# A residual-network trunk in float32: half of the down projection's low weight parts by a negated copy and an accumulating DMA

## The chip, the cores and the metric

The kernel runs on one core of one Trainium2 chip. The metric is the time of one execution in microseconds (us) on the device. Before the change it is 2249.22 us, the median of three runs (2248.68 to 2249.78).

## The reference

Two decoder layers over 256 tokens of 2048 channels, all in float32. Each layer normalises its input, projects it once for two kinds of attention, adds the output projection to the residual stream, and then adds an MLP. The change lies in the last line, the down projection of the MLP.

```python
def hybrid_layer(x, ...):
    h = rms_norm(x, attn_norm)
    proj = jnp.einsum('bsd,de->bse', h, w_in)
    ...
    mixed = jnp.concatenate([o_gla, o_sb], axis=-1)
    x = x + jnp.einsum('bse,ed->bsd', mixed, w_o)
    hm = rms_norm(x, mlp_norm)
    up = jnp.square(jax.nn.relu(jnp.einsum('bsd,df->bsf', hm, w_up)))   # 2048 -> 8192
    return x + jnp.einsum('bsf,fd->bsd', up, w_down)                    # 8192 -> 2048
```

## The kernel before

All weights (about 400 MB) stream once from HBM through SBUF. TensorE works on a float32 format with fewer bits (`F32R`), so every weight is split into a high part (the value rounded to that format) and a low part (what the rounding left). Activations are split in the same way, and a product is made of three matmuls: high by high, high activation by low weight, low activation by high weight.

`weight_parts` (L307) makes the split. It loads one **group** of weights, 1 MB, with one DMA on SP's queue into a tile `raw` of 128 partitions by 2048 float32 values (L314; three such buffers). Then it goes through the group's two halves, 128x1024 values each. For a half, ScalarE copies `raw` into `whi`, which rounds (L325), and VectorE subtracts `whi` from `raw` into `wlo` (L327, two sources). There are four buffers of `whi` and four of `wlo`, handed out in turn. It is a generator: each half is given to its caller before the next one is made.

`unit` (L332) makes a product of 256 tokens by 512 columns. It walks over four groups of weights, 512 rows each. For each half it issues 12 matmuls of 512 columns (L344 to L346), so 24 for a group. `unit_t` (L378) is the same with the columns on partitions; the up projection uses it.

`mlp_down` (L902) calls `unit` four times for a quarter of the 8192 hidden channels, once for each 512 output columns, and adds the accumulator to the residual stream on VectorE (L919). So one call is a **pass** of 16 groups. A layer has four passes, with up projections between the first three and the next, and there are two layers. The very last pass of the program writes the output and is treated apart in the change.

The order on each engine comes from the program and a scheduler in the framework. An engine takes its instructions in order. A load can be issued when its `raw` buffer is free, that is when everything that reads the former group in it is done. A `whi` or `wlo` can be written when TensorE is done with the half that had the buffer before.

Of the kernel before, what the change touches and what calls it, by code (L numbers as in the profile page):

```python
# [16 lines left out]
P = 128  # L17
# [22 lines left out]
def trunk_kernel(  # L40
# [31 lines left out]
    def nm(s):  # L72
        uid[0] += 1
        return f"{s}_{uid[0]}"
# [16 lines left out]
    def f32(ap):  # L91
        return ap.bitcast(F32)

    nc.scalar.preload_act_table_set("natural_log_exp_and_others")

# [1 line left out]
    ident = cpool.tile([P, P], F32, name="ident")  # L97
# [9 lines left out]
    def build_constants():  # L107
        nc.vector.tensor_copy(ident16, ident)

        # strictly causal mask of a diagonal block, keys on partitions: 0 where s < t  # L110
        nc.gpsimd.memset(mask16, 0.0)
        nc.gpsimd.affine_select(
            out=mask16, in_=mask16, compare_op=ALU.is_gt, fill=NEG,
            base=0, pattern=[[1, P]], channel_multiplier=-1,
        )
        # suffix sums: -1 where j >= s (j on partitions)
        tri_f, nones_f = tmp("t2", [P, P], bufs=4), tmp("t2", [P, P], bufs=4)
        nc.gpsimd.memset(tri_f, -1.0)
        nc.gpsimd.affine_select(
            out=tri_f, in_=tri_f, compare_op=ALU.is_ge, fill=0.0,  # L120
            base=0, pattern=[[-1, P]], channel_multiplier=1,
        )
        nc.vector.tensor_copy(tri, tri_f)
        nc.gpsimd.memset(nones_f, -1.0)
        nc.vector.tensor_copy(nones, nones_f)
        # 1 where s <= c and both lie in one chunk (s on partitions)
        nc.gpsimd.memset(gmask, 1.0)
        for half in range(2):
            nc.gpsimd.affine_select(
                out=gmask[half * CHUNK : (half + 1) * CHUNK, :],  # L130
                in_=gmask[half * CHUNK : (half + 1) * CHUNK, :],
                compare_op=ALU.is_ge, fill=0.0,
                base=0, pattern=[[1, CHUNK]], channel_multiplier=-1,
            )
        # scan multiplier: 0 at the start of each chunk
        nc.gpsimd.memset(reset, 1.0)
        nc.gpsimd.memset(
            reset.rearrange("p (n c) -> p n c", c=CHUNK)[:, :, 0:1], 0.0
        )
        # exp(last - cum) * k, tokens on partitions, one chunk's rows kept per entry  # L140
        nc.gpsimd.memset(kdz, 0.0)

# [1 line left out]
    NA = KT * DEPTH  # L144
# [48 lines left out]

# [1 line left out]
    xb = [xpool.tile([P, NT, 512], F32, name=f"xb{n}") for n in range(4)]  # L195
# [8 lines left out]

# [1 line left out]
    clock = [0]  # L206
# [16 lines left out]

# [1 line left out]
    def inv_rms(ss, n, width):  # L225
        """(ss / width + EPS) ** -0.5, [P, n], with one Newton step."""
        v, y, t, t2, rr = stat(n), stat(n), stat(n), stat(n), stat(n)
        nc.vector.tensor_scalar(v, ss, 1.0 / width, EPS, ALU.mult, ALU.add)
        nc.scalar.activation(y, v, AF.Ln)
        nc.scalar.activation(y, y, AF.Exp, scale=-0.5)  # L230
        nc.vector.tensor_tensor(t, y, y, ALU.mult)
        nc.vector.scalar_tensor_tensor(t2, t, -0.5, v, ALU.mult, ALU.mult)
        nc.vector.scalar_tensor_tensor(rr, t2, 1.5, y, ALU.add, ALU.mult)  # L233
        return rr

    class Operand:
        """Activations with channels on partitions: [P, 2 blocks, (high, low), T] tiles."""

# [14 lines left out]
    def norm_operand(op, n, key, l):  # L253
        """Residual block n -> operand blocks 4n.. (scaled by the gain)."""
        for h2 in range(2):
# [34 lines left out]
    def wait_on_x(n):  # L290
        """Keep the array running while the first operands arrive."""
        pw = ps_tile()
        for _ in range(n):
            nc.tensor.transpose(pw[:, :P], ident, ident)

    def row_of(col):
        """[P, NT] per-token column -> [P, T] rows, the same on every partition."""
        pb = ps_tile()
        for tt in range(NT):
            w = tmp("bc", [P, P], bufs=1)  # L300
            nc.gpsimd.tensor_copy(w, col[:, tt : tt + 1].to_broadcast([P, P]))  # L301
            nc.tensor.transpose(pb[:, tt * P : (tt + 1) * P], w, ident)
        row = tmp("row", [P, T], bufs=2)
        nc.vector.tensor_copy(row, pb[:, :T])
        return row

    def weight_parts(w2d, r0, c0, kt, width, fine=False, halves=1, order=lambda k: None):  # L307
        """kt row blocks from row r0: exact high and low parts, in pieces of row blocks."""
        full = 2048 // kt
# [3 lines left out]
        for s in range(0, kt, step):  # L313
            nc.sync.dma_start(raw[:, s : s + step, :width], src[:, s : s + step, :])  # L314
        for s in range(2):
            hk = kt // 2
            hi = wpool.tile([P, hk, full], F32R, tag="whi", name=nm("whi"), bufs=4)
# [13 lines left out]

    def unit(op, w2d, row0, c0, width, groups=(0, 1, 2, 3), hooks={}, fine=0, split=False, order=lambda i, k: None):  # L332
        """[T, width] = op @ w2d[row0 + ..., c0:c0+width], tokens on partitions."""
        acc = acc_tile()
# [15 lines left out]
        def prep(i):  # L350
            return weight_parts(
                w2d, row0 + 4 * groups[i] * P, c0, 4, width, fine=i < fine,
                halves=2 if fine else 1, order=lambda k: order(i, k),
            )
# [23 lines left out]
    def unit_t(op, w2d, c0):  # L378
        """The same for 256 columns with the columns on partitions.

        acc[:, f, 0:T] holds the high x high products, acc[:, f, T:] the others.
        """
        acc = acc_tile()
# [18 lines left out]
    def join(acc):  # L402
        """unit_t result -> [P, 2, T] on chip."""
        t = tmp("t2", [P, 2, T], bufs=4)
        nc.scalar.activation(t, acc[:, :, T:], AF.Copy)  # L405
        nc.vector.tensor_tensor(t, acc[:, :, :T], t, ALU.add)  # L406
        return t

    def head_sums(ss, src, nh):
        """Sums of squares over each 128 columns of src [P, nh * 128] -> ss [P, nh]."""  # L410
        sq = tmp("t2", [P, 512], bufs=4)
# [12 lines left out]

# [1 line left out]
    def sb_qk(acc, c, nh, h0, rst, scale, dst, wait):  # L426
        """dst[:, h0.., tok] = normalised heads of acc[:, :, c..], channels on partitions."""
        w = nh * P
# [38 lines left out]
    def sb_scores(qT, kT, h):  # L467
        """Heads h, h+1: zA [keys 0-127, (head, T)], zB [keys 128-255, (head, queries 128-255)]."""
        zA, zB = ps_tile(), ps_tile()
# [59 lines left out]
    def norm_pair(po):  # L529
        """A head pair's outputs [P, (head, tok tile, d)], each row normalised."""  # L530
        o = tmp("on", [P, 512], bufs=4)
# [6 lines left out]
    def to_operand(op, i, o, gcol):  # L538
        """Normalised outputs of a head pair -> blocks 2i, 2i+1 of the operand."""
        pt = ps_tile()  # L540
# [17 lines left out]

# [1 line left out]
    hT = Operand()  # L560
# [10 lines left out]
    for l in range(DEPTH):  # L571
# [36 lines left out]
        def sb_heads(g, qT, kT, v, first):  # L608
            """Held work for heads 4g.. ; first: wait for each pair's scores."""
            state = {}  # L610
# [18 lines left out]

        # stick-breaking heads 0-3; the gate's low-rank columns come along  # L630
        uk = unit(hT, wl, 0, C_SK, 512)
# [11 lines left out]

        # gates of the linear attention, channels on partitions
        gt = {}
# [61 lines left out]

        # stick-breaking heads 4-7
        uv = unit(hT, wl, 0, C_SV + 512, 512)
# [8 lines left out]

        # linear attention: q and k with channels on partitions, two heads a block
        eb, enb, ekd = gt["e"]  # L720
# [36 lines left out]
        def gla_pair(e, v, vc):  # L757
            """Heads 2e, 2e+1; their values are columns vc.. of v."""
            pu = ps_tile()
# [98 lines left out]

        # output projection and residual
        def residual(op, n, key, ll, ssq, acc, done):  # L860
# [16 lines left out]

        # MLP
        up = {}
# [22 lines left out]
        def mlp_down(q):  # L902
            for n in range(4):
                end = q == 3 and l + 1 == DEPTH
                ud = unit(
                    up[q], w_down[l], q * KT * P, n * 512, 512, split=(end and n == 3)
                )
# [60 lines left out]
```

## Time and profile before

| | |
|---|---|
| median of three runs | 2249.22 us |
| span of the profiled execution, first to last instruction | 2247.4 us |
| TensorE matmul busy | 2238.0 us |
| VectorE busy | 1315.8 us |
| ScalarE busy | 1085.9 us |
| GpSimd (POOL) busy | 37.7 us |
| DMA, mean | 182 GB/s |

The profile is of one execution. Its own time outside the profiler is not listed; its span stands 1.8 us under the median of the runs, which is what lies around the span. Matmul ends are modelled and overlap, so the time from one matmul's start to the next says more than the duration of one. The share of DMA is the mean share of time in which the core's 16 DMA engines were busy.

### The profile page before, as it was taken

Reading aid. Unit: us, or ns where it says so; the run is one execution under the profiler, and the core shown is the slowest. Engines: PE = TensorE matmul, PEld = TensorE weight load, DVE = VectorE, ACT = ScalarE, POOL = GpSimd, SP = SyncE. Lnnn points to the kernel's source line nnn. Section 1 sums busy time; section 2 is a strip of 40 time slices with the busy share of each in tenths; the row PEclk is TensorE's granted clock in tenths of the full one; section 3 lists DMA queues with packets and bytes.
Section 4 is the critical chain, followed back from the end, with each engine's and each line's share of the span. In section 5 each row is a group of like instructions: output and inputs, shape, how many; then the busy total and the mean of one; then the engine's idle time right before and its main releaser. Section 6 shows DMA issues by size and latency. Waiting matters only on the chain.

```text
span 2247.4 us, 28019 instructions
## 1 busy us (share of the span) xinstructions
PE 2238.0 (100%) x11436; PEld 1883.2 (84%) x11436; DVE 1315.8 (59%) x1508; ACT 1085.9 (48%) x1363; POOL 37.7 (2%) x67
## 2 busy tenths in 40 slices
PE   9999999999999999999999999999999999999999
PEld 7988778888888888888888887888888888888887
DVE  5777565666556556555557765656655554565554
ACT  5555355555345445445445553555543453454442
POOL 0020000000000000000000200000000000000000
PEclk9999999999999999999999999999999999999999
DMA  6555445665565566565546544456665655655554
GB/s 226 190 157 163 150 143 195 187 188 188 200 191 186 190 188 187 190 196 192 180 149 202 169 152 149 164 184 182 191 194 191 187 188 191 192 186 197 189 197 141
DMA packets 283622, 409.04 MB, mean 182 GB/s; under 512 B 6651, under 2 KB 162883, under 8 KB 283493
## 3 DMA queue, kind: packets, MB, share of 16 engines
q1 hardware_dynamic: 283492, 407.24, 56.6%
q8 instruction: 90, 1.47, 0.3%
q14 instruction: 40, 0.32, 0.0%
HBM read 405.12 MB, written 2.10 MB: 181 GB/s over the span
## 4 chain that ended last, share of the span: by engine, by line
PE 98%; DVE 1%; issue 0%; DMA 0%; ACT 0%; POOL 0%; SPq 0%; DVEq 0%; POOLq 0%
PE acc L391 24%; PE acc L344 19%; PE acc L346 19%; PE acc L345 19%; PE acc L395 12%; PE ps L261 1%; PE ps L806 1%; PE ps L818 1%; PE ps L765 0%; PE ps L507 0%; PE ps L453 0%; PE ps L542 0%; PE ps L471 0%; DVE wlo L327 0%; DMA raw<-in_w_in_dram 0%
## 5 line engine op out<-in xcount | busy, mean ns | idle before, releaser
L327 DVE TENSOR_TENSOR wlo<-raw,whi 128x1024 fp32r<-128x1024 f32 (+2 forms) x786 | 944.4, 1204 | 805.2 <-ACT whi L325 804.6
L325 ACT ACTIVATE whi<-raw 128x1024 fp32r<-128x1024 f32 (+2 forms) x786 | 816.4, 1041 | 1036.7 <-PE acc L346 642.8
L391 PE MATMUL acc<-act,whi 128*128 128x512 f32 x2304 | 811.2, 397 | 0.0
L344 PE MATMUL acc<-whi,act 128*128 128x512 f32 (+2 forms) x1984 | 766.6, 386 | 1.4 <-ACT act L269 1.1
L345 PE MATMUL acc<-wlo,act 128*128 128x512 f32 (+2 forms) x1984 | 760.3, 383 | 0.4 <-DVE wlo L327 0.4
L346 PE MATMUL acc<-whi,act 128*128 128x512 f32 (+2 forms) x1984 | 759.9, 383 | 0.0
L395 PE MATMUL acc<-act,wlo 128*128 128x256 f32 x2304 | 644.1, 280 | 0.0
L391 PEld LDWEIGHTS acc<-act,whi 128*128 128x128 f32 x2304 | 432.7, 188 | 104.0
L344 PEld LDWEIGHTS acc<-whi,act 128*128 128x128 f32 x1984 | 372.9, 188 | 76.5 <-issue 4.1
L395 PEld LDWEIGHTS acc<-act,wlo 128*128 128x128 f32 x2304 | 434.4, 189 | 0.4
L346 PEld LDWEIGHTS acc<-whi,act 128*128 128x128 f32 x1984 | 372.7, 188 | 73.8 <-issue 0.7
L345 PEld LDWEIGHTS acc<-wlo,act 128*128 128x128 f32 x1984 | 372.9, 188 | 71.7 <-DVE wlo L327 1.2
L406 DVE TENSOR_TENSOR t<-acc,t 128x512 f32<-128x512 f32 x72 | 49.2, 683 | 0.0
L894 DVE TENSOR_TENSOR act<-t,act 128x512 fp32r<-128x512 f32 x64 | 44.3, 692 | 6.2 <-ACT act L893 6.2
L893 ACT ACTIVATE act<-t 128x512 fp32r<-128x512 f32 x64 | 40.5, 634 | 11.8 <-PE acc L346 10.0
L888 DVE SCALAR_TENSOR_TENSOR t<-t,row 128x512 f32<-128x512 f32 x64 | 44.3, 692 | 2.2
L405 ACT ACTIVATE t<-acc 128x512 f32<-128x512 f32 x72 | 41.6, 578 | 0.0
L892 ACT ACTIVATE t<-t 128x512 f32<-128x512 f32 x64 | 39.4, 615 | 0.0
L919 DVE TENSOR_TENSOR xb<-acc,xb 128x1024 f32<-128x1024 f32 x24 | 29.4, 1224 | 9.6 <-PE acc L346 9.6
L413 DVE TENSOR_REDUCE st<-t 128x4 f32<-128x512 f32 (+1 forms) x36 | 21.6, 622 | 0.5
L301 POOL COPY bc<-st 128x128 f32<-128x128 f32 x8 | 2.6, 320 | 1149.5 <-DVE st L233 1059.9
L412 DVE TENSOR_TENSOR t<-on 128x512 f32<-128x512 f32 x16 | 11.9, 743 | 16.1 <-ACT on L532 16.1
(137 smaller groups left out, 669.4 us busy)
## 6 DMA issues: line engine op xcount, KB each, us to landing
raw<-in_w_up_dram SPq DMA_DIRECT2D x128, 1024.0 KB, 5.8
raw<-in_w_down_dram SPq DMA_DIRECT2D x128, 1024.0 KB, 5.0
raw<-in_w_in_dram SPq DMA_DIRECT2D x84, 1024.0 KB, 5.2
raw<-in_w_o_dram SPq DMA_DIRECT2D x32, 1024.0 KB, 5.1
raw<-in_w_in_dram SPq DMA_DIRECT2D x14, 512.0 KB, 6.7
raw<-in_w_in_dram SPq DMA_DIRECT2D x8, 544.0 KB, 3.9
out_dram<-xb SPq DMA_DIRECT2D x8, 256.0 KB, 2.3
xb<-in_x_dram SPq DMA_DIRECT2D x3, 512.0 KB, 7.9
```

Source lines behind the costliest of these rows:

```text
L325: newest["hi"] = nc.scalar.activation(h, r, AF.Copy).ins
L327: newest["lo"] = nc.vector.tensor_tensor(lo[:, q : q + step, :width], r, f32(h), ALU.subtract).ins
L344: nc.tensor.matmul(o, xh[:, sl], whi[:, j, :width], start=first, stop=False)
L345: nc.tensor.matmul(o, xh[:, sl], wlo[:, j, :width], start=False, stop=False)
L346: st["mm"] = nc.tensor.matmul(o, xl[:, sl], whi[:, j, :width], start=False, stop=last).ins
L391: nc.tensor.matmul(acc[:, f, :], whi[:, j, sl], op.both(k), start=(k == 0), stop=False, skip_group_check=True,)
L395: nc.tensor.matmul(acc[:, f, T:], wlo[:, j, sl], xh, start=False, stop=(k == KT - 1), skip_group_check=True,)
L405: nc.scalar.activation(t, acc[:, :, T:], AF.Copy)
L406: nc.vector.tensor_tensor(t, acc[:, :, :T], t, ALU.add)
L888: nc.vector.scalar_tensor_tensor(t, t, 0.0, nxt["row"].unsqueeze(1).to_broadcast([P, 2, T]), ALU.max, ALU.mult,)
L893: nc.scalar.activation(d[:, :, 0, :], t, AF.Copy)
L894: nc.vector.tensor_tensor(d[:, :, 1, :], t, f32(d[:, :, 0, :]), ALU.subtract)
```

## The change

For 28 of the 32 calls of `unit` in `mlp_down` (all but the last pass of the last layer), each group's **second** half is made in another way, and ahead of the first half. ScalarE rounds `raw` into `whi` as before. VectorE writes `raw` times -1 into `wlo`, which rounds too and so gives the negated high part, without reading `whi`. Then a DMA on GpSimd's queue adds `raw` to `wlo` in place, from SBUF to SBUF: raw minus high is the low part. The first half is made as before. The rest of the difference is removed comments, which shift line numbers.

```diff
-    def weight_parts(w2d, r0, c0, kt, width, fine=False, halves=1, order=lambda k: None):
+    def weight_parts(w2d, r0, c0, kt, width, fine=False, halves=1, order=lambda k: None, adder=False):
...
         for s in range(0, kt, step):
             nc.sync.dma_start(raw[:, s : s + step, :width], src[:, s : s + step, :])
+        hk = kt // 2
+        second = None
+        if adder:
+
+            hi = wpool.tile([P, hk, full], F32R, tag="whi", name=nm("whi"), bufs=4)
+            lo = wpool.tile([P, hk, full], F32R, tag="wlo", name=nm("wlo"), bufs=4)
+            r = raw[:, hk : 2 * hk, :width]
+            nc.scalar.activation(hi[:, :, :width], r, AF.Copy)
+            nc.vector.tensor_scalar(lo[:, :, :width], r, -1.0, None, ALU.mult)
+            nc.gpsimd.dma_start(f32(lo[:, :, :width]), r, accum_op=ALU.add)
+            second = (hi, lo)
         for s in range(2):
-            hk = kt // 2
+            if s and second:
+                yield second
+                continue
             hi = wpool.tile([P, hk, full], F32R, tag="whi", name=nm("whi"), bufs=4)
...
-                halves=2 if fine else 1, order=lambda k: order(i, k),
+                halves=2 if fine else 1, order=lambda k: order(i, k), adder=i in adder,
...
-                    up[q], w_down[l], q * KT * P, n * 512, 512, split=(end and n == 3)
+                    up[q], w_down[l], q * KT * P, n * 512, 512, split=(end and n == 3),
+                    adder=() if end else (0, 1, 2, 3),
```

What this does to the order is seen on VectorE in the second `unit` of the first pass. `raw_...` is a group, `wlo_...` a half, and L919 (L933 in the change) is the addition of the first `unit`'s accumulator to the residual. Before:

```order
L327 TENSOR_TENSOR wlo_4859<-raw_4856,whi_4858 128x1024
L327 TENSOR_TENSOR wlo_4875<-raw_4856,whi_4874 128x1024
L327 TENSOR_TENSOR wlo_4893<-raw_4890,whi_4892 128x1024
L919 TENSOR_TENSOR xb_96<-acc_4717,xb_96 128x1024
L327 TENSOR_TENSOR wlo_4909<-raw_4890,whi_4908 128x1024
L327 TENSOR_TENSOR wlo_4927<-raw_4924,whi_4926 128x1024
```

And in the change, from the same place:

```order
L323 TENSOR_SCALAR wlo_4863<-raw_4860 128x1024
L340 TENSOR_TENSOR wlo_4868<-raw_4860,whi_4867 128x1024
L323 TENSOR_SCALAR wlo_4898<-raw_4895 128x1024
L933 TENSOR_TENSOR xb_96<-acc_4717,xb_96 128x1024
L340 TENSOR_TENSOR wlo_4903<-raw_4895,whi_4902 128x1024
L323 TENSOR_SCALAR wlo_4933<-raw_4930 128x1024
```

Of each group's two rows the first is now the negated copy of the second half, and the other the subtraction for the first half; nothing else moves.

GpSimd had no work in this part of the program. In the change its queue holds there one DMA for each group and nothing else; the waits are for the group's load (DMAHW), for an earlier accumulating DMA (DMASW) and for the negated copy (DVE):

```order
L324 DMA wlo_4791<-raw_4788 128x1024 [waits DMAHW3_49,DVE_49]
L324 DMA wlo_4826<-raw_4823 128x1024 [waits DMAHW4_49,DVE_49]
L324 DMA wlo_4863<-raw_4860 128x1024 [waits DMAHW5_49,DMASW0_49,DVE_49]
```

And the loads on SP's queue in the same passes come to wait for accumulating DMAs as well, since those read `raw`. Before:

```order
L314 DMA raw_4786<-in_w_down_dram 128x4x512 [waits DMAHW0_49,DVE_49]
```

In the change, the fourth and the fifth load of the first pass:

```order
L314 DMA raw_4823<-in_w_down_dram 128x4x512 [waits DMAHW1_49,DMASW0_49,DVE_49]
L314 DMA raw_4860<-in_w_down_dram 128x4x512 [waits DMAHW2_49,DMASW1_49,DVE_49]
```

DMASW0 is the first accumulating DMA of the pass, DMASW1 the second: a load now follows the addition of the group three before it.

## Rows read from the trace of the kernel before

**Rows 1.** The page: span, busy time of each engine, chain by engine
```profile
span 2247.4 us, 28019 instructions
...
PE 2238.0 (100%) x11436; PEld 1883.2 (84%) x11436; DVE 1315.8 (59%) x1508; ACT 1085.9 (48%) x1363; POOL 37.7 (2%) x67
...
PE 98%; DVE 1%; issue 0%; DMA 0%; ACT 0%; POOL 0%; SPq 0%; DVEq 0%; POOLq 0%
```

**Rows 2.** Busy time by stretch, the first layer's passes 1, 2 and 3
```profile
core 0: us, PE busy (x) PEld busy (x) DVE busy (x) ACT busy (x) POOL busy (x), PEclk, DMA share, GB/s
541.00:628.00 87.00, 87.00 (x401) 72.56 (x401) 46.55 (x41) 37.10 (x38) 0.00 (x0) 1.00 0.57 191
718.00:805.00 87.00, 87.00 (x400) 72.49 (x399) 46.05 (x41) 37.11 (x38) 0.00 (x0) 1.00 0.57 190
895.00:983.00 88.00, 88.00 (x406) 73.34 (x405) 46.84 (x42) 37.11 (x38) 0.00 (x0) 1.00 0.58 192
```

**Rows 3.** TensorE in order of time, pass 2: start us, us, engine, line
```profile
738.37 0.39 PE L344 MATMUL acc<-whi,act 128*128 128x512 f32 x1
738.60 0.39 PE L345 MATMUL acc<-wlo,act 128*128 128x512 f32 x1
...
743.81 0.39 PE L344 MATMUL acc<-whi,act 128*128 128x512 f32 x1
```

**Rows 4.** Waits in pass 1: us in total, times, longest us
```profile
ACT whi L325 <- PE acc L346: 41.7, 26, 1.7
DVE wlo L327 <- ACT whi L325: 38.6, 29, 1.6
```

**Rows 5.** DMA queues of the whole program, from the page
```profile
q1 hardware_dynamic: 283492, 407.24, 56.6%
q8 instruction: 90, 1.47, 0.3%
q14 instruction: 40, 0.32, 0.0%
```

**Rows 6.** DMA between 740 and 760 us: busy tenths and GB/s, 0.5 us a slice
```profile
DMA  9998000085999970005389999600054699993000
GB/s 406 410 418 315 33 0 0 0 57 152 373 406 418 410 275 25 0 0 61 33 168 369 406 410 410 254 20 0 0 33 45 258 406 397 418 414 127 0 0 0
```

**Rows 7.** VectorE groups by shape: count | busy us, mean ns | idle before
```profile
L327 DVE TENSOR_TENSOR wlo<-raw,whi 128x1024 fp32r<-128x1024 f32 x750 | 919.3, 1228 | 785.2 <-ACT whi L325 784.6
```

**Rows 8.** DMA issues: count, KB each, median us from issue to landing
```profile
raw<-in_w_down_dram SPq DMA_DIRECT2D x128, 1024.0 KB, 5.0
...
out_dram<-xb SPq DMA_DIRECT2D x8, 256.0 KB, 2.3
...
wg<-in_w_gate_up_dram SPq DMA_DIRECT2D x2, 32.0 KB, 1.7
```

**Rows 9.** SP's queue in pass 1: what its loads waited for
```profile
SPq L314 <- DVE wlo L327: 80.3, 16, 5.2
```

More of the change, by code (lines that the diff above doesn't have):

```diff
@@ L330, in weight_parts, with unit @@
             yield hi, lo
-    def unit(op, w2d, row0, c0, width, groups=(0, 1, 2, 3), hooks={}, fine=0, split=False, order=lambda i, k: None):
+    def unit(op, w2d, row0, c0, width, groups=(0, 1, 2, 3), hooks={}, fine=0, split=False, order=lambda i, k: None, adder=()):
         acc = acc_tile()
```

## The prediction

> **What bounds the kernel now.** I read the page first. TensorE is busy for 2238.0 of 2247.4 us, and the chain that ended last is 98% TensorE [rows 1]; VectorE, the engine that the change relieves, is busy 59% of the span. Then the stretches of single passes of the down projection: in three of them TensorE is busy for every microsecond (87.00 of 87.00, 87.00 of 87.00, 88.00 of 88.00) at a granted clock of 1.00, which is the 2.4 GHz level, while VectorE is busy for about 46 us and GpSimd for none [rows 2]. The timeline of TensorE gives the beat: from one first matmul of a half to the one 24 matmuls later it takes 743.81 - 738.37 = 5.44 us, so a group takes 5.44 us and a half 2.72 us [rows 3]. Last, who waits for whom: ScalarE waits for TensorE to give a buffer back, and VectorE waits for ScalarE [rows 4]. So the weight parts are always made as early as the buffers allow, and TensorE waits for none of them. VectorE's time in these passes costs nothing now, and a cheaper VectorE can give back nothing that these rows hold.
>
> **The change part by part.** It touches 28 units of 4 groups: 112 groups, in 7 passes of 16.
>
> *VectorE.* Of each group, one subtraction of 1.228 us [rows 7] goes and one copy with one source comes. No row shows such a copy from SBUF of that size; between half of 1.228 us and the whole of it is my bound, and I take 1.2 us, the row it is nearest to. The sum doesn't move with it, since VectorE is idle for 41 of 87 us there. The wait for ScalarE's rounding goes too, and costs nothing now.
>
> *The second half now needs more steps.* Before: rounding, subtraction, ready. Now: negated copy, issue on GpSimd's queue, the transfer, its completion. The time for that is set by the buffers. The second half is now made first, so with four buffers in turn it gets the one of the second half two groups earlier. That is free when TensorE ends that group, and the new content is needed after one more group and one half: 5.44 + 2.72 = 8.16 us. The chain is 1.2 us for the copy; for issue and completion 1.7 us, which a small load of 32 KB takes on SP's queue [rows 8]; and the transfer itself. GpSimd's queue has no row here (the queues that exist are SP's loads and instruction fetches [rows 5]), so 1.7 us is a lower bound, and I keep 6 us as the upper one. With the 2.8 us from below for the transfer, the chain is 5.7 us and has 2.4 us to spare. Queued behind on GpSimd is only the next accumulating DMA, 5.44 us later.
>
> *The first half* is now made after the second and may start from the same moment on ScalarE as the second: two roundings and a subtraction of 1.228 us, within a group's time of 5.44 us. ScalarE is busy for 37 of 87 us [rows 2], or 2.3 us a group, so the first half is ready some 3.6 us after the start. It costs nothing; the cover is what is left of 5.44 us.
>
> *SP's loads* are held back. A load took its buffer when the subtraction was done [rows 9]; now it waits until the addition of the group three before has ended. In the terms above that is 5.7 us after TensorE ended a group, and a load lands 5.0 us later [rows 8], that is 10.7 us after it. Its negated copy can start when TensorE has ended the third group after, at 16.3 us. That hides it, with 5.6 us to spare.
>
> *The DMA engines.* Here the sum comes out. A group loads 1024 KB, 1.05 MB, and the 16 engines are busy 0.57 of the time [rows 2], so a load takes 0.57 x 5.44 = 3.10 us of them, and 2.34 us are free. At its best, the load runs at 406 to 418 GB/s with the engines at nine tenths or more [rows 6]: 2.56 us a load, the rest being heads and tails. The accumulating DMA has 0.52 MB to add. No row shows its price. The lower bound is one plain pass at the best rate, 1.28 us. The upper one is three passes one after the other (read the source, read the destination, write), each at the load's mean price: 3 x 1.55 = 4.65 us. An addition in place must read both operands, so 1.05 MB come in, as many bytes as a load brings: nearest to it is the load, at 2.56 to 3.10 us. I take the middle, 2.83 us. A group then needs 3.10 + 2.83 = 5.93 us of engines that have 5.44 us: 0.49 us too much.
>
> The Trainium skill, Collectives: The Full Stack, section "The bandwidth ceiling: the fold count and why AG ≠ RS ≠ AR", says that an addition inside a DMA costs double because it needs two source reads (32.35 against 62.28 GB/s there). By it the price would be twice a copy's; no run here shows it yet. The sum above stands on the rows alone.
>
> *Sum.* Each pass starts with its buffers full, and 2.4 us of slack at 0.49 us a group last for 5 groups. From then on TensorE waits 0.49 us at the first low part of each second half. 11 groups x 7 passes x 0.49 us = 38 us. Against the profiled execution that is 2247.4 + 38 = 2285 us of span; against the median, 2249 + 38 = **2287 us**, or 1.7% more. About 0.2%, 4.5 us, is the least that a measurement of this kernel tells from no change.
>
> **Rivals.**
>
> *Hidden: no change, not slower.* If the addition takes less than 2.34 us of engine time, or fills the heads and tails of the loads (2.56 + 2.56 = 5.12 us is under 5.44 us), the engines keep up, the chain of 5.7 us stays within 8.16 us, and the time is 2249 us. For it speaks that at the best rate both fit, that the two transfers sit on different queues and can fill each other's gaps [rows 6], and that the loads have 5.6 us to spare. Against it, that it asks for 94% of the engines or more in a loop in which load and addition wait for each other. 0.52 MB in 2.34 us, 224 GB/s of added data, is the point that decides. The Trainium skill, DMA: Bandwidth & Descriptors, section "Anatomy of one DMA — SWDGE (gpsimd) path", gives 2.0 us plus the bytes at 436 GB/s for a DMA of GpSimd's queue; by that an estimate for a plain copy of this size is 3.2 us from end to end, which would be hidden; no run here shows it. Chance 0.33.
>
> *Dearer.* If the passes don't overlap, 4.65 us a piece: 3.10 + 4.65 = 7.75 us a group, 2.31 us over, and the slack is gone after one group. 15 x 7 x 2.31 = 243 us, or 2492 us; at the best rate throughout (2.56 + 3.84 = 6.40 us) 15 x 7 x 0.96 = 101 us, or 2350 us. Nothing in the profile rules it out; for less speaks that reading and writing of the loads plainly overlap at 410 GB/s. Chance 0.18.
>
> *GpSimd's queue is late.* The engines keep up, but issue and completion take 6 us. The chain is 1.2 + 6 + 2.8 = 10.0 us. Two groups then take as long as this chain and one half: (10.0 + 2.72) / 2 = 6.36 us a group, 0.92 us over, and 112 x 0.92 = 103 us: 2352 us. It decides from 8.16 us on, and each microsecond beyond costs half a microsecond a group. Against it: small transfers land in 1.7 us on the other queue [rows 8]. Chance 0.10.
>
> *Faster.* A VectorE with less to do could start other work earlier. But TensorE has no idle time in the passes to give back [rows 2], and 9.4 us in the whole span [rows 1]. Only a tenth of that would be 2248 us. Chance 0.02.
>
> **How the numbers follow.** The forecast, engines overfilled at 2.34 to 3.8 us an addition, has chance 0.37, and its own range is 2254 to 2350 us. It is the likeliest by a little. Slower by over 0.2%: 0.37 + 0.18 + 0.10 = 0.65. Within 0.2%: 0.33. Faster: 0.02. The range takes in the hidden case, 2249 us, from below, and reaches up through the late queue and the cheaper half of the dear case to 2440 us, which leaves out about 0.12 above and 0.02 below.
>
> **What would show it.** Right: in the passes of the changed profile the DMA share is above 0.9 in most of the stretch and TensorE's busy time is below the stretch; the wait list names TensorE's low-part matmul behind the DMA into wlo, once a group, from about the sixth group of a pass on; a group takes about 5.9 us; the up projections keep their beat. Hidden: share about 0.9 or below, and TensorE still at 5.44 us a group. Late queue: share below 0.9, long landings, TensorE waiting all the same. The prediction is wrong if passes stay at 87 us, or if the DMA into wlo lands more than 8 us after its copy while the engines stand idle.

## The result and the profile after

The change costs almost nothing: 2252.85 us (median of 20 runs, 2250.75 to 2259.46) against 2249.06 us before (20 runs, 2248.24 to 2249.96), ratio 1.002 with an interval of 1.0014 to 1.0026. The rise of 3.8 us is real, since the interval excludes 1, but it is 0.17%, which the prediction counts as no change. Forecast were 38 us. Runs of the changed kernel also lie 8.7 us apart, those of before 1.7. The profiled run of the changed kernel took 2256.01 us, so its trace shows somewhat more loss than the median.

The page of the changed kernel: span, busy time of each engine, chain by engine, queues, two groups of instructions (count | busy us, mean ns | idle before and its releaser), issues of DMAs (count, KB, median us to landing).

```profile
span 2254.2 us, 28242 instructions
...
PE 2242.4 (99%) x11436; PEld 1885.0 (84%) x11436; DVE 1253.5 (56%) x1508; ACT 1086.3 (48%) x1363; POOL 134.5 (6%) x179
...
q1 hardware_dynamic: 283492, 407.24, 55.3%
q0 software_dynamic: 16128, 58.73, 14.1%
...
PE 87%; DMA 11%; DVE 1%; issue 0%; ACT 0%; SPq 0%; POOL 0%; DVEq 0%
...
L324 POOL DMA_DIRECT2D wlo<-raw x112 | 96.7, 863 | 1157.3 <-DVE wlo L323 1157.3
L323 DVE TENSOR_SCALAR wlo<-raw 128x1024 fp32r<-128x1024 f32 x112 | 77.7, 694 | 104.9 <-DMA raw<-in_w_down_dram 90.9
...
raw<-in_w_down_dram SPq DMA_DIRECT2D x128, 1024.0 KB, 7.8
...
wlo<-raw POOLq DMA_DIRECT2D x112, 512.0 KB, 6.8
```

Beside [rows 1], the profiled execution is 6.8 us longer, VectorE is 62.3 us lighter, and TensorE's share of the last chain fell from 98% to 87%: DMAs hold 11% of it. The queue q0 is new and carries the additions. Its 14.1% of 2254.2 us, over 112, is 2.84 us of the 16 engines an addition; forecast were 2.83. (Such a price is the time that the queue's packets took, spread over the 16 engines.) A load of the down projection now lands after 7.8 us, not 5.0 [rows 8].

The first two of the stretches of [rows 2], and the DMA engines between 740 and 760 us as in [rows 6]:

```profile
core 0: us, PE busy (x) PEld busy (x) DVE busy (x) ACT busy (x) POOL busy (x), PEclk, DMA share, GB/s
541.00:628.00 87.00, 86.73 (x396) 71.86 (x396) 36.99 (x40) 35.44 (x38) 13.05 (x15) 1.00 0.98 262
718.00:805.00 87.00, 87.00 (x400) 72.50 (x399) 37.81 (x41) 37.42 (x38) 13.30 (x16) 1.00 0.98 271
```

```profile
DMA  9999999998999999999979999999999999999998
GB/s 238 209 217 217 188 229 205 184 119 299 401 397 401 393 328 193 238 250 246 221 279 414 397 410 414 217 188 221 213 205 360 389 418 397 410 270 213 238 147 123
```

The forecast was that a pass with its engines at 0.9 and more would run slow. Here the engines stand at 0.98 throughout, the pauses between loads are gone, and TensorE still does its pass in all but a few tenths of a microsecond. Who waits, in the whole program (total us, times, longest):

```profile
ACT whi L322 <- DMA raw<-in_w_down_dram: 144.0, 49, 5.7
DVE wlo L323 <- DMA raw<-in_w_down_dram: 90.9, 51, 4.5
...
PEld acc L358 <- DMA wlo<-raw: 8.6, 12, 1.8
...
PE acc L358 <- DMA wlo<-raw: 3.4, 5, 1.4
```

ScalarE and VectorE now wait for **loads** where they waited for TensorE and for each other [rows 4]. TensorE waits for an addition a dozen times, not some 77 times. Its eleven gaps, 0.14 to 1.55 us each, add up to 5.5 us, and the matmul behind each starts another 0.11 us late: 6.7 us in all, which is the span's 6.8. In the first layer they come late in the first pass and in the third. The chain of pass 1 shows what runs late there (start us, us, what):

```profile
554.86 10.13 DMA raw<-in_w_down_dram
565.11 0.71 DVE wlo L323
565.82 0.28 issue
566.10 7.34 DMA wlo<-raw
573.50 8.05 DMA raw<-in_w_down_dram
...
582.66 8.11 DMA wlo<-raw
590.82 8.80 DMA raw<-in_w_down_dram
...
600.73 6.63 DMA wlo<-raw
607.42 8.96 DMA raw<-in_w_down_dram
...
617.49 8.10 DMA wlo<-raw
625.63 0.50 PE acc L358
```

This is a loop: load, copy, issue, addition, and then the load that takes the same `raw` buffer. With three buffers one turn must serve three groups, 3 x 5.44 = 16.32 us. The turns take 582.66 - 566.10 = 16.56, 18.07 and 16.76 us, 17.13 in the mean: 0.8 us late a turn, hidden by the lead with which a pass starts, until TensorE stops at 625.63, some 74 us into a pass of 87.

So two theories stood, called by their letters in the expectations below. **A, as predicted:** the DMA engines are short by a little, and the loop is late since they are full. **F:** the engines are fast enough, and the loop through three `raw` buffers is too long, because load and addition stretch each other.

### The profile page after: what moved, and what is told of

Read it like the earlier page. It is cut to its first block, busy times and chain, and to the rows that moved or that the text cites. A ratio compares the mean times of both kernels' runs of the same rounds, so it can differ in the third digit from the quotient of the medians.

```text
span 2254.2 us, 28242 instructions
## 1 busy us (share of the span) xinstructions
PE 2242.4 (99%) x11436; PEld 1885.0 (84%) x11436; DVE 1253.5 (56%) x1508; ACT 1086.3 (48%) x1363; POOL 134.5 (6%) x179
## 3 DMA queue, kind: packets, MB, share of 16 engines
q0 software_dynamic: 16128, 58.73, 14.1%
## 4 chain that ended last, share of the span: by engine, by line
PE 87%; DMA 11%; DVE 1%; issue 0%; ACT 0%; SPq 0%; POOL 0%; DVEq 0%
PE acc L404 24%; PE acc L357 16%; PE acc L358 16%; PE acc L359 16%; PE acc L408 12%; DMA raw<-in_w_down_dram 5%; DMA wlo<-raw 5%; PE ps L261 1%; PE ps L819 1%; PE ps L831 1%; DVE wlo L323 1%; PE ps L778 0%; PE ps L520 0%; PE ps L466 0%; PE ps L555 0%
## 5 line engine op out<-in xcount | busy, mean ns | idle before, releaser
L340 DVE TENSOR_TENSOR wlo<-raw,whi 128x1024 fp32r<-128x1024 f32 (+2 forms) x674 | 806.8, 1200 | 742.6 <-ACT whi L338 741.9
L338 ACT ACTIVATE whi<-raw 128x1024 fp32r<-128x1024 f32 (+2 forms) x674 | 697.6, 1038 | 805.1 <-PE acc L359 404.2
L322 ACT ACTIVATE whi<-raw 128x1024 fp32r<-128x1024 f32 x112 | 119.2, 1064 | 239.8 <-DMA raw<-in_w_down_dram 144.0
L324 POOL DMA_DIRECT2D wlo<-raw x112 | 96.7, 863 | 1157.3 <-DVE wlo L323 1157.3
L323 DVE TENSOR_SCALAR wlo<-raw 128x1024 fp32r<-128x1024 f32 x112 | 77.7, 694 | 104.9 <-DMA raw<-in_w_down_dram 90.9
L933 DVE TENSOR_TENSOR xb<-acc,xb 128x1024 f32<-128x1024 f32 x24 | 29.3, 1222 | 23.3 <-PE acc L359 23.3
```

What stands on the lines that cost most here:

```text
L322: nc.scalar.activation(hi[:, :, :width], r, AF.Copy)
L323: nc.vector.tensor_scalar(lo[:, :, :width], r, -1.0, None, ALU.mult)
L324: nc.gpsimd.dma_start(f32(lo[:, :, :width]), r, accum_op=ALU.add)
L338: newest["hi"] = nc.scalar.activation(h, r, AF.Copy).ins
L340: newest["lo"] = nc.vector.tensor_tensor(lo[:, q : q + step, :width], r, f32(h), ALU.subtract).ins
```

## The experiments

Each was timed beside the kernel before on the same chip. The diffs are against the changed kernel unless said.

### Half of the additions

```diff
-                    adder=() if end else (0, 1, 2, 3),
+                    adder=() if end else (0, 2),
```

> Only every other group (0 and 2 of each unit's four) is made with the adding DMA, so 56 additions instead of 112. Theory A, the 16 DMA engines: in the changed kernel's passes they are 0.98 busy, a load costs about 2.7 us of them and an addition about 2.7, together hardly less than the 5.44 us of a group; with half the additions a group needs about 4.1 us, the share falls to about 0.77, TensorE waits for no DMA, 2249 us (2247 to 2251). Rival B, the second half made first and copied costs time on ScalarE or VectorE: half of the loss stays, 2251 us, and TensorE waits for whi or for wlo from VectorE. Rival C, issue on GpSimd's queue is slow: half of the loss stays, TensorE waits for the DMA into wlo although the engines have idle time.

2255.63 us (7 runs) against 2248.83, ratio 1.0026 (1.0015 to 1.0037): half of the additions cost as much as all of them. Pass 1 by stretch, then TensorE's wait for additions in the whole program:

```profile
541.00:628.00 87.00, 85.53 (x390) 70.08 (x389) 40.72 (x40) 36.34 (x37) 7.01 (x8) 1.00 0.79 218
```

```profile
PEld acc L358 <- DMA wlo<-raw: 8.0, 12, 1.8
```

The DMA engines between 594 and 614 us (0.5 us a slice), and the additions that landed there:

```profile
DMA  9999999973019599999988899999998300009469
...
wlo<-raw POOLq DMA_DIRECT2D x2, 512.0 KB, 10.4
```

The share is 0.79 and TensorE waits all the same, so A falls in the form "engines that are full all the time make it late". The two additions of this stretch land after 10.4 us (the median of all 56 is 7.2) although an addition costs 2.66 us of engines (q0's 6.6% of 2253.9 us, over 56). The chain shows one of them:

```profile
588.35 10.87 DMA raw<-in_w_down_dram
...
600.34 10.85 DMA wlo<-raw
```

SP issues in order: a load that waits for an addition holds back the load behind it. In this pass SP's loads wait 8 times for an addition, 81.6 us, and 3 times for a subtraction, 7.4 us. So two loads leave together when an addition ends (at 598.9 and 599.4 us in the trace), and the next addition, at 600.34, shares the engines with 2 MB. The engines are full from 601 to 609.5 us and nearly idle from 598.5 to 600 us and for 2 us after. The addition is late because it stands in a bunch; over the whole pass the engines have time left.

### The copy without its addition

The adding DMA is left out, so the second halves' low parts hold only the negated high parts and the sum is missing.

```diff
-            nc.gpsimd.dma_start(f32(lo[:, :, :width]), r, accum_op=ALU.add)
```

> The order and the negated copy of the change, without the adding DMA, whose sum is left out (the low part of the second half then holds the negated high part). Theory A, the DMA engines are the whole story: 2249 us (2247 to 2250), and with VectorE's busy time about 60 us lower nothing is gained, since TensorE never waited for it. Rival B, order and copy cost: about 2253 us. Rival D, the lighter VectorE gives something back that the additions hide: under 2246 us.

2248.71 us (11 runs) against 2248.83, ratio 0.9999 (0.9991 to 1.0008). The other order and the copy cost nothing, and VectorE's 60.6 us less of work (1255.2 against 1315.8) gives nothing back. All of the loss hangs on the DMA.

### The same DMA as a plain copy

`raw` is copied over `wlo`; the sum is again left out.

```diff
-            nc.gpsimd.dma_start(f32(lo[:, :, :width]), r, accum_op=ALU.add)
+            nc.gpsimd.dma_start(f32(lo[:, :, :width]), r)
```

> The DMA on GpSimd's queue copies raw over wlo instead of adding it, so the sum is left out; bytes, queue, issue and waits stay. Theory A, an addition is dear because it reads two operands: the transfer costs about 1.35 us of the engines instead of 2.7, share in the passes about 0.75, landing about 4 us, no waits, 2249 us (2247 to 2251). Rival C, queue and fixed costs of GpSimd's DMAs are what is felt: packets as long as with the addition, landings near 6.8 us, and 2252 us or more.

2249.24 us (11 runs), ratio 1.0001 (0.9992 to 1.001). Landing and share came higher than expected, 5.5 us and 0.81 in pass 1, and TensorE waits for no DMA. Queue and landing, from the page:

```profile
q0 software_dynamic: 16128, 58.73, 6.9%
...
wlo<-raw POOLq DMA_DIRECT2D x112, 512.0 KB, 5.5
```

6.9% of 2247.2 us over 112 is 1.38 us a copy, against 2.84 us an addition of as many bytes: 2.05 times. The path (GpSimd's queue, the waits, the loads held back) is the same and costs nothing here; the loss comes only with the longer transfer.

### Both halves by addition

```diff
...
-            second = (hi, lo)
...
+                made[s] = (hi, lo)
+            yield made[0]
+            yield made[1]
+            return
```

(with the copy and the addition in a loop `for s in (0, 1)`)

> Both halves of each group by negated copy and adding DMA, 224 additions. Theory A: 2.7 + 2 x 2.75 = 8.2 us of engines a group against 5.44, 2.75 us too much; about one group of each pass is covered by slack, 15 x 7 x 2.75 = 290 us, so about 2540 us (2450 to 2600), share 0.97 or more in the passes. Rival E, not the engines but the loop through three raw buffers sets the pace (load, copy, addition, then the next load may start): (9 + 1.6 + 10) / 3 = 6.9 us a group, about 2400 us, with the share under 0.93. Rival C, GpSimd's issues one after the other are too slow: TensorE waits, landings long, share under 0.9.

2518.83 us (4 runs), ratio 1.1201 (1.1179 to 1.1222), +270 us. Here A holds: two additions of 2.74 us (q0's 24.4% of 2516.4 us, over 224) and a load of 2.56 us at its best rate [rows 6] are 8.0 us of engines in a group of 5.44; the mean group took 5.44 + 270/112 = 7.85 us. Pass 1 to 620 us, and a stretch in it:

```profile
541.00:620.00 79.00, 66.58 (x278) 51.65 (x277) 20.19 (x28) 24.04 (x26) 17.77 (x20) 0.94 1.01 250
566.00:569.00 3.00, 3.00 (x9) 2.32 (x8) 1.29 (x2) 1.42 (x2) 0.42 (x1) 0.50 0.97 315
```

The share is 1.01, and TensorE is short by 12.4 of 79 us. From 566 to 569 us its granted clock is 0.50, the 1.2 GHz level; a wait for an addition, with 2.6 us between two matmuls' starts, lies just ahead, and the matmuls start 0.43 us apart there, not 0.23. From 578 to 582 us it is 0.50 again, after a wait of 5.0 us. So these two waits cost more than themselves.

### A fourth raw buffer

The room comes from two of the 19 activation buffers.

```diff
-    apool = ctx.enter_context(tc.tile_pool(name="acts", bufs=19))
+    apool = ctx.enter_context(tc.tile_pool(name="acts", bufs=17))
...
-        raw = wpool.tile([P, kt, full], F32, tag="raw", name=nm("raw"))
+        raw = wpool.tile([P, kt, full], F32, tag="raw", name=nm("raw"), bufs=4)
```

> The change with four raw buffers instead of three (two activation buffers of 4 KB fewer make the room). With half the additions the loss had stayed although the engines were idle for a fifth of the time, so theory A (engines full) is doubtful. Theory F: a load may start only when the addition three groups earlier has ended, it then shares the engines with the next addition, both come late, and the negated copy waits for the load (it did 51 times, 91 us); a fourth buffer opens that loop. F: 2249 us (2247 to 2251), VectorE's copy waits for TensorE instead of the load, TensorE for no DMA. A: 2252 us or more, TensorE still waits for the DMA into wlo late in the passes, with a share of 0.98 or more.

2249.80 us (11 runs) against 2248.93, ratio 1.0003 (0.9994 to 1.0012): the loss is gone, as far as the interval tells (it leaves room for up to 2.7 us). Two of the stretches again and ten groups' time in the middle of pass 1; the waits for loads and additions in the whole program; the queues; and VectorE in pass 1 in order of time, with the idle time before and what ended it:

```profile
541.00:628.00 87.00, 87.00 (x400) 72.60 (x399) 38.27 (x42) 37.62 (x39) 13.91 (x16) 1.00 0.99 272
895.00:983.00 88.00, 88.00 (x404) 73.30 (x404) 38.48 (x43) 37.78 (x39) 13.79 (x16) 1.00 0.99 273
...
560.00:614.40 54.40, 54.40 (x241) 45.05 (x240) 21.46 (x23) 21.23 (x20) 8.58 (x10) 1.00 1.04 285
```

```profile
DVE wlo L323 <- DMA raw<-in_w_down_dram: 4.5, 6, 1.4
...
PEld acc L358 <- DMA wlo<-raw: 0.5, 2, 0.3
```

```profile
q1 hardware_dynamic: 283492, 407.24, 55.5%
q0 software_dynamic: 16128, 58.73, 13.7%
```

```profile
565.42 0.69 DVE L323 TENSOR_SCALAR wlo<-raw 128x1024 fp32r<-128x1024 f32 x1 [0.17 <-PE acc L358]
...
570.86 0.69 DVE L323 TENSOR_SCALAR wlo<-raw 128x1024 fp32r<-128x1024 f32 x1 [0.17 <-PE acc L358]
573.81 1.23 DVE L933 TENSOR_TENSOR xb<-acc,xb 128x1024 f32<-128x1024 f32 x1 [2.25 <-PE acc L359]
```

This decides for F. The engines move a load and an addition every 5.44 us, not 5.93, and TensorE waits for additions only twice, 0.5 us in the whole program. The share is 0.99 over the stretch and 1.04 in the middle of the pass: it adds up the packet times of both queues, which run side by side, so a share of 1 does not mean that the engines can take no more. The load is out of the loop (the copy waits for one 6 times, not 51), and a copy starts every 5.44 us, when TensorE gives a buffer back.

The last fence corrects another number. The accumulator is read at 573.81 us, when TensorE has ended a group, its second half included. The copy at 570.86 started 2.95 us earlier, so it waited for the end of a **first** half. It is the buffer of the first half two groups earlier that the copied half gets: the buffers go to the next half as they come free, and not strictly in turn. From there to its use are four halves: 10.88 us, not the 8.16 us of the prediction. With 7.8 us of landing (the median of this run) and 1 us of copy and issue it fits.

### The fourth buffer with half of the additions

Against the run with half of the additions:

```diff
-    apool = ctx.enter_context(tc.tile_pool(name="acts", bufs=19))
+    apool = ctx.enter_context(tc.tile_pool(name="acts", bufs=17))
...
-        raw = wpool.tile([P, kt, full], F32, tag="raw", name=nm("raw"))
+        raw = wpool.tile([P, kt, full], F32, tag="raw", name=nm("raw"), bufs=4)
```

> Every other group by addition, as in the first experiment, with four raw buffers. F: 2249 us (2247 to 2251) where three buffers gave 2255.6. Rival G: what makes the addition late is that two loads are issued back to back just before it and it gets a third of the engines, about 10 us to landing whatever the buffers: still 2253 us or more, with landings of 9 us or more and the copy waiting for no load.

2253.72 us (11 runs), ratio 1.0021 (1.0012 to 1.003). The copy waits for no load any more, and yet the loss stays. The chain in pass 2:

```profile
766.69 0.70 DVE wlo L323
...
767.68 10.47 DMA wlo<-raw
...
778.19 0.50 PE acc L358
```

Copy, issue and transfer are 11.5 us, more than the 10.88 us there are. The addition still starts right behind two loads (issued from 766.88 us on). So with two additions in four groups the transfer's own delay is enough, without the loop. With all additions the loads are spaced by them, and with half of them they come in pairs: by these traces, that is why fewer cost no less.

### The kernel before with the fourth buffer

The control. Against the kernel before:

```diff
-    apool = ctx.enter_context(tc.tile_pool(name="acts", bufs=19))
+    apool = ctx.enter_context(tc.tile_pool(name="acts", bufs=17))
...
-        raw = wpool.tile([P, kt, full], F32, tag="raw", name=nm("raw"))
+        raw = wpool.tile([P, kt, full], F32, tag="raw", name=nm("raw"), bufs=4)
```

> Control: the kernel before with four raw buffers and two activation buffers fewer, no additions. All theories: 2249 us (2247.5 to 2250.5); if it is more, that much of the two runs beside it is the missing activation buffers.

2249.01 us (11 runs), ratio 0.9999 (0.999 to 1.0008). The buffers by themselves move nothing.

### The natural order

The second half is made after the first, as before the change.

```diff
-        if adder:
...
         for s in range(2):
-            if s and second:
-                yield second
+            if s and adder:
+                hi = wpool.tile([P, hk, full], F32R, tag="whi", name=nm("whi"), bufs=4)
...
+                nc.gpsimd.dma_start(f32(lo[:, :, :width]), r, accum_op=ALU.add)
+                yield hi, lo
                 continue
```

> The change with the second half made after the first, as the kernel before has it; copy, addition and three raw buffers stay. The four buffers give the second half 8.16 us in either order, so F and A: about 2252 us (2250 to 2257), as the change. Rival H, making it first buys the addition time: clearly more than the change, 2260 us or more, with the DMA into wlo waited for in every pass.

2319.59 us (5 runs), ratio 1.0297 (1.0275 to 1.0319). The hope that this order would serve as well is refuted: in it the copy gets the buffer of the second half two groups earlier and has the 8.16 us that the prediction gave to the change. From the chain in pass 1:

```profile
563.64 0.24 PE acc L355
...
563.91 0.71 DVE wlo L323
...
564.90 9.51 DMA wlo<-raw
...
574.45 0.50 PE acc L355
```

From the release, at the end of the matmul of 563.64, to the use it takes 10.6 us, 2.4 too many. The share of pass 1 is 0.93, below what the fourth buffer's run carried without loss.

### The natural order with the fourth raw buffer

```diff
-        raw = wpool.tile([P, kt, full], F32, tag="raw", name=nm("raw"))
+        raw = wpool.tile([P, kt, full], F32, tag="raw", name=nm("raw"), bufs=4)
```

(and two activation buffers fewer; against the run with the natural order)

> The natural order (second half after first) with four raw buffers. The eighth run went against F's number: 2319.6 us where about 2252 was expected. Theory F amended: the loop through the raw buffers is load, copy, issue, addition, and in the natural order the first half's rounding and subtraction (about 2.3 us) stand between the load and the copy, so a turn of three groups is 2.3 us longer, 0.77 us a group. A fourth buffer gives a turn 5.44 us more, so F: 2249 to 2254 us, ScalarE and VectorE waiting for TensorE and not for loads. Rival H, it is the start of the second half in the wlo buffers that comes too late: the time stays above 2300 us and TensorE waits for the DMA into wlo as before.

2322.58 us (4 runs), ratio 1.0322 (1.0299 to 1.0346). No gain, so late loads alone are not what holds this order. ScalarE's roundings, which waited 43 times for loads of the down projection with three buffers (103.6 us), no longer wait for any; TensorE's waits for additions are as before: 70.2 us in 44 waits at its weight loads, against 67.5 in 43. What is left in the trace is the time from the buffer's release to its use.

### Both halves with the fourth raw buffer

```diff
-        raw = wpool.tile([P, kt, full], F32, tag="raw", name=nm("raw"))
+        raw = wpool.tile([P, kt, full], F32, tag="raw", name=nm("raw"), bufs=4)
```

(and two activation buffers fewer; against the run with both halves)

> Both halves by addition with four raw buffers. With three the engines were full (share 1.01 in the first pass) and the time 2518.8 us. If the engines are the limit there, as A had it for that run, the fourth buffer changes little: 2480 to 2530 us, share 1.0. If the loop through the raw buffers was the limit there too (F): clearly less, under 2450 us.

2479.37 us (4 runs), ratio 1.1032 (1.0996 to 1.1068). Against the kernel before on the same chip the loss is 229 us where it was 270; the share of pass 1 stays at 1.02. So the loop held some 40 us of this loss, and the rest stays: where the engines are really short, a buffer helps little. The time lies by 1 us under the expected range.

### The natural order with a fifth wlo buffer

```diff
-    apool = ctx.enter_context(tc.tile_pool(name="acts", bufs=19))
+    apool = ctx.enter_context(tc.tile_pool(name="acts", bufs=18))
...
-                lo = wpool.tile([P, hk, full], F32R, tag="wlo", name=nm("wlo"), bufs=4)
+                lo = wpool.tile([P, hk, full], F32R, tag="wlo", name=nm("wlo"), bufs=5)
```

(at both places where a `wlo` is taken; against the natural order)

> The natural order with five wlo buffers instead of four (one activation buffer fewer), three raw buffers. Theory F's loop didn't explain the natural order: a fourth raw buffer left it at 2322.6 us. Theory J: the buffers go to the next half in the order in which they come free, so in the change's order a second half gets the buffer of a first half and has four halves, 10.9 us, from its copy to its use; in the natural order it has three, 8.2 us, and the chain of 1 us and 6 to 9 us of landing doesn't fit. A fifth buffer gives 10.9 us to the natural order too. J: 2250 to 2258 us, as the change. Rival F': the first half's rounding and subtraction ahead of the copy are what costs: still above 2300 us.

2306.15 us (4 runs), ratio 1.0248 (1.0232 to 1.0264): the loss is 55 us where it was 71, and the fifth buffer was to bring almost all of it back. VectorE in pass 1, and the rounding that its subtraction waited for:

```profile
586.87 1.22 DVE L337 TENSOR_TENSOR wlo<-raw,whi 128x1024 fp32r<-128x1024 f32 x1 [3.85 <-ACT whi L335]
588.01 0.69 DVE L323 TENSOR_SCALAR wlo<-raw 128x1024 fp32r<-128x1024 f32 x1
```

```profile
585.78 1.06 ACT L335 ACTIVATE whi<-raw 128x1024 fp32r<-128x1024 f32 x1 [2.77 <-DMA raw<-in_w_down_dram]
```

The copy no longer waits for its buffer, but it stands in VectorE's queue directly behind the subtraction, which waits for ScalarE's `whi`. That rounding had waited for a load here, as 47 roundings of this run did (101.5 us); earlier in the pass, at 567.64 and 573.08 us, it waited for TensorE to give one of the four `whi` buffers back. The time, and a copy that always stands right behind the subtraction, are what the rival F' expected. In these traces late loads hold the natural order back with three `raw` buffers, and the buffers of the halves with four; neither kind of buffer alone brings the time back. The natural order with a fourth `raw` and a fifth `wlo` together, or with a fifth `whi`, was not run, so the cause of its loss stays argued.

### Half of the additions, fourth raw, fifth wlo

```diff
-    apool = ctx.enter_context(tc.tile_pool(name="acts", bufs=17))
+    apool = ctx.enter_context(tc.tile_pool(name="acts", bufs=16))
...
-            lo = wpool.tile([P, hk, full], F32R, tag="wlo", name=nm("wlo"), bufs=4)
+            lo = wpool.tile([P, hk, full], F32R, tag="wlo", name=nm("wlo"), bufs=5)
```

(at both places where a `wlo` is taken; against half of the additions with the fourth raw buffer)

> Every other group by addition, with four raw and five wlo buffers (three activation buffers fewer). With four raw buffers alone 2253.7 us were left, TensorE waiting for additions that land 10 us and more after issue, since two loads go out just before each. J: 2.7 us more from copy to use cover it, 2249 us (2247.5 to 2251), landings as long as before. Rival: the time stays at 2253 us or more, so something else than the landing is waited for.

2254.68 us (11 runs) against 2250.70, ratio 1.0014 (1.0004 to 1.0023). Missed as well, if less clearly: TensorE's waits at its weight loads fall from 6.1 us to 4.0, and the time doesn't return to that of before. The copies stand behind subtractions here too. What holds the rest of the loss with half of the additions is not shown.

## Why the prediction was wrong

**The forecast.** 2287 us was put down; the time is 2252.85, inside the range, and the case that came nearest is the rival *Hidden* (0.33), not the forecast (0.37). By the prediction's own sign it was wrong: passes stayed at 87 us. *Hidden* is right that the engines keep up, though it put their share at about 0.9, and it too counted on 5.6 us to spare for the loads.

**The step that failed** is the sum "3.10 + 2.83 = 5.93 us of engines that have 5.44 us: 0.49 us too much". The addition's term was right: 2.84 us in the changed kernel, 2.75 with four `raw` buffers (13.7% of 2247.7 us, over 112), 2.66 in the run with half of the additions. The load's term and the adding up were not. 3.10 us is what a load's packets take when it runs alone. Beside additions the load queue's packets took 55.5% of 2247.7 us, against 56.6% of 2247.4 before, 24.5 us less: 2.88 us a load. With 2.75 us for the addition that is 5.63 us, still more than 5.44, and yet a group took 5.44 us in the run with four `raw` buffers. So packet times of two queues can't be set against the clock as if one excluded the other: in the changed kernel, from 740 to 760 us, the two queues' shares are 62.2% and 43.2%, more than the whole. The rival's working, bytes at the best rate, came nearer: 2.56 + 2.56 = 5.12 us fits, and three times 2.56, 7.68 us, is near the 7.5 to 7.85 us a group that load and two additions took with both halves (5.44 us and 229 or 270 us over 112). The prediction dismissed it since 94% of the engines in a loop seemed too much.

**Then 0.49 us a group on 11 groups of 7 passes** had nothing to stand on: no run shows a shortage of 0.49 us a group. The 3.8 us that did come have another cause.

**"5.6 us to spare" for SP's loads** was wrong, and this is the cause of the 3.8 us. The working took the 5.0 us of a load that has the engines to itself, and 5.7 us from release to the end of an addition. Beside additions, a load takes 8.0 to 9.0 us in the loop of pass 1 and an addition 6.6 to 8.1, 1 us of copy and issue ahead of it: 17.1 us a turn where 16.32 are free. A step that was taken as hidden became the late one. That the fourth buffer alone brings the time back (1.0003), and changes nothing in the kernel before (0.9999), shows it.

**8.16 us from the buffer's release to its use** is 10.88 us in the change's order. Two wrong terms thus cancelled, by luck: the chain takes 7.8 to 9.1 us, not 5.7, and would often not have fitted into 8.16. The natural order, which by its trace has 8.16 us, lost 71 us, and a fourth `raw` buffer did not help it; that the shorter time is the whole reason is argued and not shown, since the fifth `wlo` buffer brought only 15 us back. The rival *GpSimd's queue is late* described such a lateness, and gave +103 us; but the issue takes 0.28 us in the chain, and what was long is the time from issue to landing beside loads.

**Right:** a lighter VectorE gives nothing (2248.71 us without the addition); the first half, now later, costs nothing; the addition costs as much as reading both operands. *Dearer* is ruled out by 2.84 us an addition, *Faster* by the run without the addition. Too high, without consequence: the copy takes 0.694 us, not 1.2. Not foreseen: each issue keeps GpSimd busy for 0.86 us, which nobody waits for.

**The two rules cited.** The Trainium skill, Collectives: The Full Stack, section "The bandwidth ceiling: the fold count and why AG ≠ RS ≠ AR", says of the additions of a ReduceScatter between cores that they halve the rate because each needs two source reads. The runs agree, for an addition within one core: 2.84 us against 1.38 us of engines for the same bytes on the same queue, 2.05 times, and 1.9 times with the 2.66 us of the run with half of the additions. The Trainium skill, DMA: Bandwidth & Descriptors, section "Anatomy of one DMA — SWDGE (gpsimd) path", gives 2.0 us plus the bytes at 436 GB/s, from which the prediction made its estimate of 3.2 us from end to end for a plain copy. The run with the plain copy shows a median of 5.5 us, beside loads; the shortest of its 112 copies landed after 2.9 us.

**Left open:** why runs of the changed kernel spread over 8.7 us was not followed up; nor was the natural order tried with more than one kind of buffer added at a time.

## What to carry to other kernels

Two transfers that each look too dear for what is left of the engines may fit once both stand in the queues: cost the pair by the bytes read at the rate at which the engines run when full, not by adding one stream's mean share to another's. Then give both their durations under sharing, and walk each buffer's whole round (release, load, use, next release) against the beat; here one more buffer, and not fewer bytes, took the loss away. Fewer of a transfer is not always cheaper, and the order in which halves are made changes how long each may take.

## What the runs showed of the hardware

- With four `raw` buffers the 16 DMA engines kept up with TensorE at a share of 0.99 over passes of 87 us and 1.04 in the middle of one, where TensorE was busy all the time: the shares of two queues add up to more than 1.
- An accumulating DMA from SBUF to SBUF of 0.52 MB takes 2.66 to 2.84 us of the 16 engines, a plain copy of as many bytes 1.38 us. In the changed kernel it lands after 4.8 to 10.3 us, 6.8 in the median; right behind two loads it took 10.4 us, in a pass with a mean share of only 0.79.
- VectorE's copy with one source takes 694 ns for 128x1024 float32 values in SBUF, its subtraction with two 1228 ns [rows 7].
- With both halves by addition, TensorE ran at the granted clock of 0.50 (1.2 GHz) after waits of 2.6 and 5.0 us, from 566 to 569 and from 578 to 582 us, and its matmuls started 0.43 us apart instead of 0.23.
